# Wider score tiles, a full-array product for the low part of K, and the experts' sums moved by half an item

## The chip, the cores and the metric

The kernel runs on one core of a Trainium2 chip. The metric is the device time of one execution in microseconds. The core has a matrix engine (TensorE, PE in the rows; its weight loads are PEld), VectorE (DVE), ScalarE (ACT), GpSimd (POOL) and SyncE (SP, whose queue issues most DMA transfers); PSUM is the memory that TensorE writes its products to, SBUF the one that all engines work in.

## What is computed

One layer of a hybrid decoder on 2048 tokens of width 1024: a token mixer of three head groups, then a mixture of 32 experts. Three pieces of the reference matter here. The index scores and the sparse attention (n_sel is 256 keys of up to 2048):

```python
logits = jnp.einsum('bqhd,bsd->bqhs', iqb, ikf) * DSA_IDX_DIM ** -0.5      # 8 index heads of 32
score = jnp.einsum('bqh,bqhs->bqs', iwb, jax.nn.relu(logits))
score = jnp.where(admissible[None], score, -jnp.inf)
_, sel = lax.top_k(score, n_sel)
...
s = jnp.einsum('bqhd,bqkhd->bhqk', qb, kg) * DSA_HEAD_DIM ** -0.5          # 4 heads of 64
p = jax.nn.softmax(jnp.where(valid[:, None], s, -jnp.inf), axis=-1)
return jnp.einsum('bhqk,bqkhd->bqhd', p, vg)
```

and the experts, of which every token takes two, with the residual and the final norm:

```python
hid = jax.nn.silu(xb @ w_gate[e]) * (xb @ w_up[e])
return hid @ w_down[e]
...
y = jnp.zeros((T, D), out.dtype).at[tok_sorted].add(contrib)     # contrib: out times the token's weight
...
x = x + gt2 * hier_moe(...)
return rms_norm(x, final_norm_g)
```

## The kernel before

Matrix products are made in a reduced format of f32; for accuracy an operand is split into a high part (ScalarE's copy into that format) and a low part (VectorE's or POOL's difference from it).

*Index scores* (L241 to L264, 60 to 420 us of the span). For a block b of 128 queries the keys up to (b + 1) x 128 are taken in segments of 512. For each pair of segments (GS = 2) and each of 8 heads: one product into a PSUM tile pi (three of 512 columns), a Relu by ScalarE into rl (three of 512) and a multiply-add by VectorE into the sums sb (L253), for each segment by itself; the first head adds to eps, a tiny slope over the keys. Scores of earlier blocks are woven into the projections of later ones; the last blocks stand alone at the end.

*Sparse attention* (L1469 to L1640, 1280 to 1645 us). Query blocks go in pairs; dsa_prep loads the queries of a pair (qd), makes their high part qh on ScalarE, and a tile Q of which, for head parity e, one half of the partitions holds the high part and the other the low part (POOL's difference). dsa_scores multiplies it by KH, which holds the high part of K in both halves (L1533): high times high plus low times high, on all 128 rows. The third term, high times K's low part KL, uses the 64 partitions of that head alone (L1534), so its product has 64 rows. VectorE adds the mask and takes the maximum (L1535), ScalarE makes the exponentials (L1542); dsa_values transposes them (L1565), splits them (ph L1573, pl L1574) and multiplies them by V. Five of the eight 512 KB rows of w_out are loaded meanwhile (NWP = 5), the rest in the output stage.

*Experts* (1930 to 3036 us). The 32 experts' lists have fixed capacities CAP: 18 big items (more than 128 tokens, in two blocks of n rows) alternate with 14 small ones (one block). Step r of the loop works on item r's gate and up products and on item r - 1's down product. A big item does gate and up in two halves of its hidden units (gate_up with c = 0 and 1), and its weights come in 512 KB pieces (slots wraw, 11 of them) that ScalarE and VectorE split into wh and wl (L1904, L1905); a small item multiplies the raw pieces (L1928). In between stands down() for the item before: for the column halves c and the blocks j, 12 products into a PSUM tile pd, VectorE's multiplication by the token's weight and gt2 in place (L1986), and VectorE's addition into part (L1987), the sum so far of these tokens, which POOL gathered from the table yp_d (L1975). POOL scatters part back to yp_d (L1989). finish(), written at the end of the step, squares part on ScalarE (L2000), takes a reciprocal root (two VectorE operations, L61 and L62, and twelve small ones on POOL, L64 to L67), and multiplies part by it and by the final norm's gain into ot on VectorE (L2005), which POOL scatters to the output (L2006). For a token's first expert the sum goes to yp_d only and for its second to the output only; the other scatter leaves that row out. A gather of yp_d waits for the scatters written ahead of it, and a scatter for the one before.

The code is in program order; a scheduler that places instructions by their dependences and expected times sets the order on each engine, so an engine's row is not the order of the code. Engines and queues then run their rows strictly in turn.

## Time and profile before

| | us |
|---|---|
| median of 3 runs | 3036.46 |
| lowest and highest | 3034.36, 3040.60 |
| profiled execution | 3037.47 |
| its span | 3035.6 |
| TensorE busy | 2461.5 (81%) |
| TensorE weight loads | 1884.2 (62%) |
| VectorE busy | 2057.4 (68%) |
| ScalarE busy | 1363.2 (45%) |
| POOL busy | 1074.6 (35%) |

The profile is one execution of the program. An engine is busy while one of its instructions runs; the idle time ahead of an instruction is put down to what released it last ("issue" is a wait for which the profile shows no releaser). The granted clock of TensorE is a share of full speed; its mean over the execution is 0.876.

### The profile page before, as it was taken

Reading aid. Unit: us, or ns where it says so; the run is one execution under the profiler, and the core shown is the slowest. Engines: PE = TensorE matmul, PEld = TensorE weight load, DVE = VectorE, ACT = ScalarE, POOL = GpSimd, SP = SyncE. Lnnn points to the kernel's source line nnn. Section 1 sums busy time; section 2 is a strip of 40 time slices with the busy share of each in tenths; the row PEclk is TensorE's granted clock in tenths of the full one; section 3 lists DMA queues with packets and bytes.
Section 4 is the critical chain, followed back from the end, with each engine's and each line's share of the span. In section 5 each row is a group of like instructions: output and inputs, shape, how many; then the busy total and the mean of one; then the engine's idle time right before and its main releaser. Section 6 shows DMA issues by size and latency. Waiting matters only on the chain.

```text
span 3035.6 us, 39091 instructions
## 1 busy us (share of the span) xinstructions
PE 2461.5 (81%) x12571; PEld 1884.2 (62%) x12571; DVE 2057.4 (68%) x4570; ACT 1363.2 (45%) x2467; POOL 1074.6 (35%) x1123
## 2 busy tenths in 40 slices
PE   4998877778377899789997999488888878887785
PEld 3766645777366677556665788455566655665574
DVE  6588977989879755457676566565566665654575
ACT  2578876663122244356555222243344443443452
POOL 2111133436554332255533354213233333332333
PEclk9999878898667789869998999689999989998888
DMA  7222264433321343353213433687888878887781
GB/s 211 85 91 79 87 224 131 112 132 124 109 84 50 110 144 112 94 147 109 88 49 114 160 133 127 182 250 239 264 258 251 253 234 271 252 245 208 216 235 53
DMA packets 372283, 479.44 MB, mean 158 GB/s; under 512 B 84828, under 2 KB 271356, under 8 KB 371814
## 3 DMA queue, kind: packets, MB, share of 16 engines
q1 hardware_dynamic: 334501, 421.83, 44.5%
q0 software_dynamic: 37568, 55.05, 6.7%
q8 instruction: 100, 1.64, 0.2%
q14 instruction: 114, 0.93, 0.1%
HBM read 385.75 MB, written 112.23 MB: 164 GB/s over the span
## 4 chain that ended last, share of the span: by engine, by line
PE 34%; DVE 11%; DMA 9%; issue 9%; POOL 5%; ACT 3%; SPq 0%; POOLq 0%; ACTq 0%; DVEq 0%
PE pg L1928 6%; DMA wraw<-in_exp_w_down_dram 2%; PE pt L1565 2%; PE ps L1534 2%; DVE wl L1905 2%; PE pw L167 2%; PE pw L166 2%; PE pw L165 2%; DMA part<-yp_d,ix 2%; DMA wraw<-in_exp_w_up_dram 1%; ACT wh L1904 1%; PE ps L1533 1%; PE pd L165 1%; PE pd L167 1%; PE pd L166 1%
## 5 line engine op out<-in xcount | busy, mean ns | idle before, releaser
L1904 ACT ACTIVATE wh<-wraw 128x1024 fp32r<-128x1024 f32 x272 | 285.0, 1054 | 251.2 <-DMA wraw<-in_exp_w_down_dram 93.6
L1905 DVE TENSOR_TENSOR wl<-wraw,wh 128x1024 fp32r<-128x1024 f32 x272 | 330.4, 1220 | 96.7 <-ACT wh L1904 91.9
L1954 PE MATMUL pg<-xT,wh 128*128 128x416 f32 (+10 forms) x1152 | 337.2, 371 | 31.4 <-DVE ga__19052 L1961 5.6
L1928 PE MATMUL pg<-wraw,xT 128*120 128x512 f32 (+9 forms) x448 | 228.2, 670 | 143.5 <-DVE ga__25810 L1961 18.6
L1956 PE MATMUL pg<-xT,wl 128*128 128x208 f32 (+10 forms) x1152 | 288.2, 250 | 0.0
L1928 PEld LDWEIGHTS pg<-wraw,xT 128*120 128x120 f32 (+9 forms) x448 | 86.1, 198 | 276.9 <-issue 114.7
L440 POOL TENSOR_TENSOR xx<-xr,xx 128x1024 fp32r<-128x1024 f32 x64 | 161.7, 2528 | 266.0 <-ACT xx L439 247.0
L1954 PEld LDWEIGHTS pg<-xT,wh 128*128 128x128 f32 x1152 | 230.2, 200 | 40.5 <-DVE ga__19052 L1961 5.8
L1956 PEld LDWEIGHTS pg<-xT,wl 128*128 128x128 f32 x1152 | 233.8, 203 | 0.0
L253 DVE SCALAR_TENSOR_TENSOR sb<-rl,iws,sb 128x512 f32<-128x512 f32 (+3 forms) x266 | 202.1, 808 | 27.3 <-ACT rl L252 23.7
L252 ACT ACTIVATE rl<-pi,iwa 128x512 f32<-128x512 f32 (+3 forms) x304 | 179.1, 653 | 22.4 <-DVE sb L253 16.8
L1863 POOL DMA_INDIRECT xg<-h_d,ix x50 | 53.4, 1068 | 350.7 <-PE pt L1881 329.7
L165 PE MATMUL pp<-xx,w 128*128 128x256 f32 x512 | 154.7, 303 | 21.5 <-ACT ft L486 11.3
L165 PE MATMUL pd<-wh,hid 128*104 128x512 f32 (+17 forms) x400 | 160.6, 402 | 6.6 <-DVE part L1987 4.0
L1989 POOL DMA_INDIRECT yp_d<-part,ix x50 | 70.9, 1418 | 258.8 <-DVE part L1987 189.9
L166 PE MATMUL pd<-wl,hid 128*104 128x512 f32 (+17 forms) x400 | 158.1, 395 | 0.0
L167 PE MATMUL pd<-wh,hid 128*104 128x512 f32 (+17 forms) x400 | 157.5, 394 | 0.0
L166 PE MATMUL pp<-xx,w 128*128 128x256 f32 x512 | 152.2, 298 | 3.1 <-POOL xx L440 3.1
L167 PE MATMUL pp<-xx,w 128*128 128x256 f32 x512 | 151.8, 298 | 0.8 <-POOL w L467 0.8
L250 PE MATMUL pi<-iks,iqs 128*128 128x512 f32 (+3 forms) x304 | 129.2, 478 | 22.2 <-ACT rl L252 19.2
L1535 DVE CUSTOM_DVE_ANT_0 pr<-ps,mk 128x512 f32<-128x512 f32 (+3 forms) x160 | 95.6, 606 | 61.7 <-PE ps L1534 43.5
L165 PE MATMUL pj<-w,xx 128*128 128x512 f32 (+1 forms) x256 | 100.0, 392 | 39.7 <-DVE ot L211 19.5
(1075 smaller groups left out, 7021.8 us busy)
## 6 DMA issues: line engine op xcount, KB each, us to landing
wraw<-in_exp_w_gate_dram SPq DMA_DIRECT2D x128, 512.0 KB
wraw<-in_exp_w_up_dram SPq DMA_DIRECT2D x128, 512.0 KB
wraw<-in_exp_w_down_dram SPq DMA_DIRECT2D x128, 512.0 KB
xr<-hT_d SPq DMA_DIRECT2D x64, 512.0 KB
w<-in_ada_w_dram SPq DMA_DIRECT2D x64, 256.0 KB
w<-in_ada_w_dram SPq DMA_DIRECT2D x16, 512.0 KB
xi<-in_x_dram SPq DMA_DIRECT2D x16, 512.0 KB
hT_d<-ht SPq DMA_DIRECT2D x16, 512.0 KB
```

Source lines behind the costliest of these rows:

```text
L165: TE.matmul(ps, st[0], mv[0], start=(k == first), stop=False, **kw)
L166: TE.matmul(ps, st[0], mv[1], start=False, stop=False, **kw)
L167: TE.matmul(ps, st[1], mv[0], start=False, stop=(k == last), **kw)
L250: TE.matmul(pi[:, :sl], iqs[:, h, i * P:(i + 1) * P], iks[:, s0:s0 + sl], start=True, stop=True)
L252: S.activation(rl[:, :sl], pi[:, :sl], AF.Relu, scale=iwa[:, b, h:h + 1])
L253: V.scalar_tensor_tensor(sb[:, s0:s0 + sl], rl[:, :sl], iws[:, b, h:h + 1], (eps if h == 0 else sb)[:, s0:s0 + sl], op0=OP.mult, op1=OP.add)
L440: G.tensor_sub(xx[1][-1], xr, xx[0][-1].bitcast(F32))
L1904: S.activation(wh, w, AF.Copy)
L1905: V.tensor_sub(wl, w, wh.bitcast(F32))
L1928: TE.matmul(pgs[a][:C], xT[:, kk], wp[2 * i + a][:, k], start=(kk == 0), stop=(kk == KD - 1))
L1954: TE.matmul(pgs[m], wh[:, k, ws], xT[:, i * 4 + k], start=(i + k == 0), stop=False, skip_group_check=True)
L1956: TE.matmul(pgs[m][:, 0], wl[:, k, ws], xT[:, i * 4 + k, 0], start=False, stop=(i + k == 4), skip_group_check=True)
```

## The change

*Scores.* A group of up to 1024 keys is one PSUM tile and one rl tile, two of each; the two products of 512 columns write its halves, and Relu and multiply-add run over the whole width. The modulation's small PSUM tile pr moves into the slot of the projections' tile pp.

```diff
-                for j, (s0, sl) in enumerate(segs[g0:g0 + GS]):
-                    pi = s1p.tile([P, 512], F32, name="pi", bufs=3)
-                    TE.matmul(pi[:, :sl], iqs[:, h, i * P:(i + 1) * P], iks[:, s0:s0 + sl], start=True, stop=True)
-                    rl = ts_.tile([P, 512], F32, name="rl", bufs=RLB)
-                    S.activation(rl[:, :sl], pi[:, :sl], AF.Relu, scale=iwa[:, b, h:h + 1])
-                    V.scalar_tensor_tensor(
-                        sb[:, s0:s0 + sl], rl[:, :sl], iws[:, b, h:h + 1],
-                        (eps if h == 0 else sb)[:, s0:s0 + sl], op0=OP.mult, op1=OP.add)
+                pi = s1p.tile([P, GS * 512], F32, name="pi", bufs=2)
+                for s0 in range(0, gl, 512):
+                    sl = min(512, gl - s0)
+                    TE.matmul(pi[:, s0:s0 + sl], iqs[:, h, i * P:(i + 1) * P], iks[:, g0 + s0:g0 + s0 + sl], start=True,
+                              stop=True)
+                rl = ts_.tile([P, GS * 512], F32, name="rl", bufs=RLB)
+                S.activation(rl[:, :gl], pi[:, :gl], AF.Relu, scale=iwa[:, b, h:h + 1])
+                V.scalar_tensor_tensor(sb[:, gs], rl[:, :gl], iws[:, b, h:h + 1], (eps if h == 0 else sb)[:, gs],
+                                       op0=OP.mult, op1=OP.add)
```

*Sparse attention.* After Q is made, the halves of qh that don't belong to the head are set to zero on POOL; with them the low product takes all 128 rows of KL, of which 64 are multiplied by zeros. qh has two buffers, and NWP falls from 5 to 4.

```diff
-            qh = da.tile([P, 2, 2, 2 * P], F32R, name="qh", bufs=1)
+            qh = da.tile([P, 2, 2, 2 * P], F32R, name="qh", bufs=2)
...
                 G.tensor_sub(Q[l_, e], qd[l_, e], qh[l_, e].bitcast(F32))
+                G.memset(qh[l_, e].bitcast(F32), 0.0)
...
-                    TE.matmul(ps[:, :sl], q_[hs], KL[hs, p_, s0:s0 + sl], start=False, stop=True)
+                    TE.matmul(ps[:, :sl], qz_, KL[:, p_, s0:s0 + sl], start=False, stop=True)
```

*Experts.* down() writes its products into an SBUF tile y (two buffers) and adds nothing. partial() gathers part (three buffers in place of two). add(), half an item later, adds part to y over the full width, tied behind the current item's last hid operation, scatters y, squares y into part and makes the root. finish(), another half item later, multiplies y by root and gain into part and scatters that. The buffers of xg fall from 4 to 3, and the tiles jk and ot are gone.

```diff
-                V.scalar_tensor_tensor(pd[:n], pd[:n], pl[:n, j, 3:4], gt2r[:n, cs], op0=OP.mult, op1=OP.mult)
-                V.tensor_add(parts[j][:n, cs], pd[:n], parts[j][:n, cs])
+                V.scalar_tensor_tensor(ys[j][:n, cs], pd[:n], pl[:n, j, 3:4], gt2r[:n, cs], op0=OP.mult, op1=OP.mult)
+        return ys
...
+            a = V.tensor_add(y[:n], y[:n], part[:n])
+            if after is not None:
+                tc.add_manual_dep(a.ins, after.ins.name, ORDER, reason="products first")
             G.indirect_dma_start(out=yp_d[:, :], out_offset=bass.IndirectOffsetOnAxis(ap=ix[:n, 1, j:j + 1], axis=0),
-                                 in_=part[:n], in_offset=None, bounds_check=T - 1, oob_is_err=False)
+                                 in_=y[:n], in_offset=None, bounds_check=T - 1, oob_is_err=False)
...
-            V.scalar_tensor_tensor(ot[:n], part[:n], rs[:n, j:j + 1], fgr[:n], op0=OP.mult, op1=OP.mult)
+            V.scalar_tensor_tensor(part[:n], y[:n], rs[:n, j:j + 1], fgr[:n], op0=OP.mult, op1=OP.mult)
...
+        if fin is not None:
+            finish(*fin)
         if r:
-            fin = down(sts[r - 1], hid, weights(es_[r - 1], 4))
+            parts = partial(sts[r - 1])
+        if r + 1 < NE:
+            xTn, todo = transpose(CAP[r + 1], sts[r + 1], (r + 1) % 2)
...
+            ys = down(sts[r - 1], hid, weights(es_[r - 1], 4))
         if r < NE:
-            rest()
+            after = rest()
             for f_ in todo:
                 f_()
             if not few:
-                hs.append(gate_up(CAP[r], xT, weights(es_[r], 2), 1))
+                h1, after = gate_up(CAP[r], xT, weights(es_[r], 2), 1)
+                hs.append(h1)
             xT = xTn
             hid = hs
         if r:
-            finish(*fin)
+            fin = sts[r - 1], ys, parts, add(sts[r - 1], ys, parts, after)
+    finish(*fin)
```

How this moves VectorE's row is shown for the big item of 2 x 96 tokens and the small one of 108 that follows it. First the end of the big item's down product, beside the small item's hid and the next item's transposed inputs xT; wl are splits of weight pieces. Before:

```order
L1986 SCALAR_TENSOR_TENSOR pd<-pd,pl_18886,gt2r 96x512
L1939 TENSOR_TENSOR hid<-pt,hid 128x4x108
L1987 TENSOR_TENSOR part<-pd,part 96x512
L1886 TENSOR_TENSOR xT<-pt,xT 128x4x88
L1905 TENSOR_TENSOR wl<-wraw,wh 128x1024
L1986 SCALAR_TENSOR_TENSOR pd<-pd,pl_18886,gt2r 96x512
L1886 TENSOR_TENSOR xT<-pt,xT 128x4x88
L1987 TENSOR_TENSOR part<-pd,part 96x512
L1886 TENSOR_TENSOR xT<-pt,xT 128x4x88
L1905 TENSOR_TENSOR wl<-wraw,wh 128x1024 x2
```

Now:

```order
L1983 SCALAR_TENSOR_TENSOR y<-pd,pl_18386,gt2r 96x512
L1908 TENSOR_TENSOR wl<-wraw,wh 128x1024
L1983 SCALAR_TENSOR_TENSOR y<-pd,pl_18386,gt2r 96x512
L1942 TENSOR_TENSOR hid<-pt,hid 128x4x108
L1889 TENSOR_TENSOR xT<-pt,xT 128x4x88
L2001 TENSOR_TENSOR y<-y,part 96x1024
L1889 TENSOR_TENSOR xT<-pt,xT 128x4x88 x2
L2001 TENSOR_TENSOR y<-y,part 96x1024
L1908 TENSOR_TENSOR wl<-wraw,wh 128x1024 x2
```

The two sums, which followed each product, stand as full-width additions behind all four products and behind hid and the first xT. Next, what follows in VectorE's row: the start of the root (sx, rs_i, rs_y), the norm, and the first ga, a sum that frees the PSUM tiles of the next big item's first half. Before:

```order
L2001 TENSOR_SCALAR sx<-sx 128x2
L61 TENSOR_SCALAR rs_i<-sx 128x2
L62 TENSOR_SCALAR rs_y<-rs_i 128x2
L1905 TENSOR_TENSOR wl<-wraw,wh 128x1024
L2005 SCALAR_TENSOR_TENSOR ot<-part,rs_y,fgr 96x1024 x2
L1961 TENSOR_TENSOR ga__22383<-ga__22383,pg_22349 128x176
L1905 TENSOR_TENSOR wl<-wraw,wh 128x1024
```

Now:

```order
L2010 TENSOR_SCALAR sx<-sx 128x2
L61 TENSOR_SCALAR rs_i<-sx 128x2
L62 TENSOR_SCALAR rs_y<-rs_i 128x2
L1908 TENSOR_TENSOR wl<-wraw,wh 128x1024
L1964 TENSOR_TENSOR ga__21841<-ga__21841,pg_21807 128x176
L2007 MEMSET sx 128x2
L2017 SCALAR_TENSOR_TENSOR part<-y,rs_y,fgr 96x1024 x2
L1964 TENSOR_TENSOR ga__21841<-ga__21841,pg_21808 128x176
L1908 TENSOR_TENSOR wl<-wraw,wh 128x1024 x2
```

The norm (now part, from y) still follows the start of the root; one ga and one operation on sx have moved ahead of it. Last, the small item's end, while the next big item's second half (the later ga) runs. Before, from the small item's second product on:

```order
L1986 SCALAR_TENSOR_TENSOR pd<-pd,pl_18887,gt2r 108x512
L1905 TENSOR_TENSOR wl<-wraw,wh 128x1024
L1987 TENSOR_TENSOR part<-pd,part 108x512
L1905 TENSOR_TENSOR wl<-wraw,wh 128x1024
L2001 TENSOR_SCALAR sx<-sx 128x2
L61 TENSOR_SCALAR rs_i<-sx 128x2
L62 TENSOR_SCALAR rs_y<-rs_i 128x2
L1905 TENSOR_TENSOR wl<-wraw,wh 128x1024
L1961 TENSOR_TENSOR ga__22593<-ga__22593,pg_22559 128x176
L2005 SCALAR_TENSOR_TENSOR ot<-part,rs_y,fgr 108x1024
L1905 TENSOR_TENSOR wl<-wraw,wh 128x1024
```

Now, from the end of that big item's second half on:

```order
L1967 TENSOR_TENSOR ga__22055<-ga__22055,ga__22094 128x2x176
L1969 TENSOR_TENSOR hid<-ga__22055,hid 128x2x176
L2001 TENSOR_TENSOR y<-y,part 108x1024
L2010 TENSOR_SCALAR sx<-sx 128x2
L61 TENSOR_SCALAR rs_i<-sx 128x2
L62 TENSOR_SCALAR rs_y<-rs_i 128x2
L2007 MEMSET sx 128x2
L2017 SCALAR_TENSOR_TENSOR part<-y,rs_y,fgr 108x1024
L1934 TENSOR_TENSOR sg<-sg,pg_22145 112x512
```

The small item's sum, root and norm have moved from the middle of the big item to behind its last hid operation, and stand ahead of sg, the next small item's first operation on VectorE.

## Rows read from the trace of the kernel before

**Rows 1.** Windows by stage: length, busy us by engine, clock, DMA share, GB/s

```profile
60.00:420.00 360.00, 317.49 (x1517) 230.63 (x1518) 284.50 (x495) 266.38 (x544) 70.49 (x91) 0.90 0.28 92
...
1280.00:1645.00 365.00, 333.41 (x1660) 233.53 (x1660) 238.67 (x759) 209.00 (x420) 170.82 (x152) 0.86 0.33 95
...
1930.00:3036.00 1106.00, 886.50 (x4420) 646.17 (x4420) 670.64 (x1073) 447.47 (x717) 355.16 (x584) 0.89 0.78 231
```

**Rows 2.** Windows, the last stretch of the scores

```profile
365.00:420.00 55.00, 40.07 (x71) 19.10 (x71) 51.22 (x70) 45.67 (x75) 13.99 (x11) 0.57 0.47 155
```

**Rows 3.** Groups by line and shape, 60 to 425 us: busy, mean ns, idle

```profile
L253 DVE SCALAR_TENSOR_TENSOR sb<-rl,iws,sb 128x512 f32<-128x512 f32 x196 | 161.1, 865 | 18.5 <-ACT rl L252 17.0
...
L253 DVE SCALAR_TENSOR_TENSOR sb<-rl,iws,eps 128x512 f32<-128x512 f32 x28 | 21.1, 766 | 3.9 <-ACT rl L252 3.9
```

**Rows 4.** Instructions on the tile part, the experts: ns min/median/max

```profile
L2005 DVE SCALAR_TENSOR_TENSOR ot<-part,rs_y,fgr x50: 1274/1281/1290, 2024.1 to 3019.9; 104x1024 f32<-104x1024 f32 x8, 88x1024 f32<-88x1024 f32 x7, 120x1024 f32<-120x1024 f32 x5, 96x1024 f32<-96x1024 f32 x4
```

**Rows 5.** Chain of waits, 1440 to 1640 us: shares by line

```profile
by line: PE pt L1565 20.6%; PE ps L1534 18.9%; PE ps L1533 13.7%; PE po L1556 12.8%; PE po L1555 11.7%; PE ps L137 3.5%; PE pf L1584 3.4%; ACT ph L1573 2.7%; DVE pl L1574 2.0%; POOL KL L1343 1.9%; DVE on L1630 1.8%; ACT pr L1542 1.1%; issue
```

**Rows 6.** The low product's line L1534: idle us, times, by cause

```profile
  issue: 30.5, 121
```

**Rows 7.** Timeline 1560 to 1566 us: start, us, instruction, idle before it

```profile
1562.64 0.39 PE L1533 MATMUL ps<-KH,Q 128*128 128x512 f32 x1
...
1562.96 0.18 PEld L1534 LDWEIGHTS ps<-KL,Q 64*128 64x128 f32 x1 [0.25 <-issue]
...
1563.39 0.42 PEld L1565 LDWEIGHTS pt<-ident,pr 128*128 128x128 f32 x4 [0.25 <-issue]
```

**Rows 8.** Timeline of TensorE, 2262 to 2266 us, a big item's down products

```profile
2263.68 0.40 PE L167 MATMUL pd<-wh,hid 128*96 128x512 f32 x1
2263.92 0.39 PE L165 MATMUL pd<-wh,hid 128*96 128x512 f32 x1
```

**Rows 9.** Groups by line and shape, POOL, whole span

```profile
L290 POOL MEMSET wst<- 128x576 f32 x1 | 0.6, 568 | 0.0
```

**Rows 10.** Waits of VectorE, 1980 to 2990 us: us, times, longest

```profile
DVE sg L1931 <- PE pg L1928: 94.0, 13, 9.3
DVE ot L2005 <- POOL rs_y L67: 90.4, 26, 10.5
DVE wl L1905 <- ACT wh L1904: 79.1, 79, 9.3
DVE part L1987 <- issue: 29.7, 7, 12.4
...
DVE part L1987 <- DMA part<-yp_d,ix: 13.1, 6, 5.7
```

**Rows 11.** The page's costliest groups, small items' gate and up products

```profile
L1928 PE MATMUL pg<-wraw,xT 128*120 128x512 f32 (+9 forms) x448 | 228.2, 670 | 143.5 <-DVE ga__25810 L1961 18.6
```

**Rows 12.** Timeline of VectorE, one pair from 2268 us, and a late one

```profile
2272.68 0.68 DVE L1987 TENSOR_TENSOR part<-pd,part 96x512 f32<-96x512 f32 x1
...
2283.73 0.06 DVE L1997 MEMSET sx<- 128x2 f32 x1 [3.15 <-POOL rs_t L65]
...
2285.12 2.48 DVE L2005 SCALAR_TENSOR_TENSOR ot<-part,rs_y,fgr 96x1024 f32<-96x1024 f32 x2
...
2311.07 1.28 DVE L2005 SCALAR_TENSOR_TENSOR ot<-part,rs_y,fgr 104x1024 f32<-104x1024 f32 x1 [2.60 <-POOL rs_y L67]
...
2754.77 0.69 DVE L1987 TENSOR_TENSOR part<-pd,part 124x512 f32<-124x512 f32 x1 [12.41 <-issue]
```

**Rows 13.** Timeline of POOL, second scatter early, both scatters late

```profile
2279.38 1.56 POOL L1989 DMA_INDIRECT yp_d<-part,ix  x1 [2.82 <-DVE wl L1905]
...
2719.47 1.16 POOL L1989 DMA_INDIRECT yp_d<-part,ix  x1 [0.78 <-DVE part L1987]
...
2729.67 1.16 POOL L1989 DMA_INDIRECT yp_d<-part,ix  x1 [7.48 <-DMA yp_d<-part,ix]
```

**Rows 14.** Timeline of TensorE, the next small item's products

```profile
2313.81 4.54 PE L1928 MATMUL pg<-wraw,xT 128*108 128x512 f32 x10 [1.54 <-DVE ga__22035 L1961]
```

More of the change, by code (lines that the diff above doesn't have):

```diff
@@ L114, in modulate @@
         return acc
-    pr = mps.tile([P, 16], F32, name="pr")
     def modulate_end(q, acc):
@@ L1464, in body @@
     WOK = (0, 1, 2, 5, 6, 7, 3, 4)
-    NWP = 5
+    NWP = 4
     def wo_row(pool, k, **kw):
@@ L1965, in gate_up @@
         S.activation(hid[:, 0], gas[0], AF.Copy)
-        V.tensor_sub(hid[:, 1], gas[0], hid[:, 0].bitcast(F32))
-        return hid
+        return hid, V.tensor_sub(hid[:, 1], gas[0], hid[:, 0].bitcast(F32))
     def down(st, hid, wp):
         n, nb, pl, ix, xgs = st
-        parts = []
-        for j in range(nb):
-            part = mx_.tile([P, D], F32, name="part", bufs=PB)
-            G.indirect_dma_start(out=part[:n], out_offset=None, in_=yp_d[:, :],
-                                 in_offset=bass.IndirectOffsetOnAxis(ap=ix[:n, 0, j:j + 1], axis=0))
-            parts.append(part)
+        ys = [mx_.tile([P, D], F32, name="y", bufs=YB) for j in range(nb)]
         for c in range(2):
@@ L1985, in down, with partial @@
                     mm3(pd[:n], [hid[k // 2][:, z, k % 2, js] for z in range(2)], w, k, 3)
-                V.scalar_tensor_tensor(pd[:n], pd[:n], pl[:n, j, 3:4], gt2r[:n, cs], op0=OP.mult, op1=OP.mult)
-                V.tensor_add(parts[j][:n, cs], pd[:n], parts[j][:n, cs])
-        for j, part in enumerate(parts):
+                V.scalar_tensor_tensor(ys[j][:n, cs], pd[:n], pl[:n, j, 3:4], gt2r[:n, cs], op0=OP.mult, op1=OP.mult)
+        return ys
+    def partial(st):
+        n, nb, pl, ix, xgs = st
+        parts = []
+        for j in range(nb):
+            part = mx_.tile([P, D], F32, name="part", bufs=PB)
+            G.indirect_dma_start(out=part[:n], out_offset=None, in_=yp_d[:, :],
+                                 in_offset=bass.IndirectOffsetOnAxis(ap=ix[:n, 0, j:j + 1], axis=0))
+            parts.append(part)
+        return parts
@@ L1989, in down, with add @@
+    def add(st, ys, parts, after=None):
+        n, nb, pl, ix, xgs = st
+        for j, (y, part) in enumerate(zip(ys, parts)):
+            a = V.tensor_add(y[:n], y[:n], part[:n])
+            if after is not None:
+                tc.add_manual_dep(a.ins, after.ins.name, ORDER, reason="products first")
             G.indirect_dma_start(out=yp_d[:, :], out_offset=bass.IndirectOffsetOnAxis(ap=ix[:n, 1, j:j + 1], axis=0),
-                                 in_=part[:n], in_offset=None, bounds_check=T - 1, oob_is_err=False)
@@ L2001, in finish @@
         V.tensor_scalar(sx, sx, 1.0 / D, EPS, op0=OP.mult, op1=OP.add)
[L2002 to L2005 removed]
+        return rsqrt_(mx_, sx, 2, "rsf", eng=G)
+    def finish(st, ys, parts, rs):
+        n, nb, pl, ix, xgs = st
+        for j, (y, part) in enumerate(zip(ys, parts)):
+            V.scalar_tensor_tensor(part[:n], y[:n], rs[:n, j:j + 1], fgr[:n], op0=OP.mult, op1=OP.mult)
@@ L2044, in body @@
     ahead(1)
-    hid = [None, None]
+    hid, fin = [None, None], None
     for r in range(NE + 1):
+        after = None
         if r < NE:
@@ L2099, in body @@
             rest()
-            finish(*down(st, hid, weights(e, 4)))
+            parts = partial(st)
+            ys = down(st, hid, weights(e, 4))
+            finish(st, ys, parts, add(st, ys, parts))
     es.close()
```

49 lines of the change are left out of this document (21 added, 28 removed).

## The prediction

> **What bounds the kernel now.** I read the table by stage first, then, for each stage that the change touches, the idle time by what ended it, and last the timeline of one repetition. By stage [rows 1] no engine is the bound throughout. The index scores (60 to 420 us) keep TensorE busy for 317.5 of 360 us and VectorE for 284.5; in their last stretch, where little but scores is left, VectorE is busy for 51.2 of 55 us, TensorE for 40.1 at a granted clock of 0.57 [rows 2]. The sparse attention (1280 to 1645) is TensorE's: 333.4 of 365 us against 238.7 on VectorE [rows 1], and over 1440 to 1640 the chain of waits names products and transposes of TensorE for over 80% of the time, L1534 and L1533 for a third [rows 5]. The experts (1930 to 3036) are bound by nothing that a busy share shows (TensorE 886.5, VectorE 670.6 of 1106 us, the DMA engines 78%): they run on a ring. A weight piece has to be split by ScalarE (wh) and VectorE (wl) before its slot is free for the next load, and VectorE takes its instructions in order, so any wait in its row delays loads. TensorE stands before a small item's products (L1928) for 143.5 us in all [rows 11]. VectorE's own waits there are for the norm's reciprocal root from POOL (ot, 90.4 us in 26 waits), for wh (79.1 us) and for gathered sums (part, 29.7 and 13.1 us) [rows 10].
>
> **Part 1, scores by 1024 keys.** Blocks 2 to 15 now make 38 segments of up to 512 keys, times 8 heads 304 Relus and 304 multiply-adds; in groups of up to 1024 they make 22, times 8 is 176. So 128 pairs become one instruction on each of the two engines; the products stay 304. A 512-wide multiply-add takes 766 ns where it reads eps and 865 elsewhere [rows 3], a 1024-wide one of the experts 1281 [rows 4]: two against one save 2 x 0.766 - 1.28 = 0.25 us. Two successive 1024-wide ones take 2.48 us [rows 12], so neighbours overlap by some 0.08 us; counted from start to start, a pair saves 0.17. That is 128 x 0.17 = 22 us of VectorE time, 32 at most, nothing at least. Only the last stretch is VectorE's alone: it holds the last two blocks, 32 pairs, 5 us. Before it TensorE is busier than VectorE and its products don't change, so of the other 17 us I take a third, 5. ScalarE saves about as much but is behind both. The tiles for it, 2 of 1024 for 3 of 512, hold more keys but are handed over in larger steps, which could cost as much as a quarter of what is saved. **-10 us, from -25 to +5.** The modulation's small tile that moves into a slot of the projections: 0 to 1 us, taken as 0.
>
> **Part 2, the low part of K on the whole array.** A pair of 512-wide products now runs so: L1533 starts at 1562.64, the weight load of L1534 only at 1562.96 with 0.25 us of "issue" before it, the next instruction's at 1563.39, again behind 0.25 us of issue [rows 7]: 0.75 us for the pair. The 64-row form has such an idle before it 121 times, 30.5 us [rows 6]. Full-array products of the same 512 columns in the experts start every 0.24 us [rows 8], so a pair would be 0.47 and save 0.28 us; 160 pairs make 45 us of TensorE. The zero rows that it now multiplies add no columns. TensorE is on the chain for 85% of the stretch [rows 5], 38 us; behind it come VectorE's splitting (pl) and ScalarE's ph, which I let end a sixth of what is gained. **-32 us, from -45 to -10.** The Trainium skill (TensorEngine Tiling, Overview and Key Properties) speaks both ways here: a contraction of 64 rows or less is said to gain up to 2x from row tiles that run side by side, which would make the old form the better one, and a change of tiling mode is said to drain the engine. No row here shows two of the 64-row products together, and the idle on both sides of L1534 is what a drain would look like; by the first sentence alone the term would be 0.
>
> The price of the zeros: 16 memsets of 64x512 on POOL. The nearest row, a memset of 128x576, took 568 ns [rows 9]: 9 us on an engine busy for 171 of 365 us [rows 1]. The low product of a block pair's first head waits for one; only the stage's start can feel it, +0.5 us, 8 at most if each pair did. The second qh buffer is paid for with one w_out row that is now loaded and split at the start of the output stage: 512 KB, at the 95 to 231 GB/s of the stages on either side [rows 1] 2 to 6 us, mostly beside other loads, +2. **Together +3.**
>
> **Part 3, experts.** Per block of tokens VectorE's two products in PSUM and two adds (0.68 us each, [rows 12]) become two products into the SBUF tile y and one full-width add. The nearest row for that is ot, 1281 ns over the same 1024 columns with two SBUF operands [rows 4]: 1.28 against 1.36, nothing. The Trainium skill (SBUF — State Buffer, Who interferes with whom) has a rule against such an add: a VectorE instruction with two SBUF inputs contends with a POOL instruction that reads SBUF. If it stretched 50 adds as the common multiply-add of the scores is stretched against the one on eps, 865 to 766 [rows 3], it would cost 50 x 0.17 = 8 us of VectorE. In the experts, beside POOL's own work, ot took 1274 to 1290 ns in all 50 [rows 4], so the sum has none of it.
>
> What counts is where things stand in the rows. *Big item (two blocks).* Its first sum was ready at 2273.36, after the third product and its add; the second scatter started at 2279.38, then came POOL's twelve root steps, and ot at 2285.12 behind a wait of 3.15 us [rows 12, 13]. Now all four products, the small item's hid and one xT stand ahead of the first add, with splits between them: worked out from the durations it ends near 2278.0, 4.6 us later. The second scatter still waits for the first to land, and the norm still stands close behind the root's start in VectorE's row (the order shows it; writing finish half an item later did not move it there). The second scatter's wait of 2.82 us was ended by VectorE's row and not by the landing [rows 13], so some of the 4.6 is slack: ot starts 3.5 us later in early pairs, up to 4.4 in late ones where the scatter is slow. *Small item (one block).* Its two adds (1.36), its stall for the root (2.60) and its ot (1.28, [rows 12]) leave the stretch between the big item's two halves and go behind hid of the second half, where VectorE idles until the next small item's gate products end (sg waits 94.0 us in 13 times, some 7 each [rows 10]). That takes 5.2 us out of the path to the next small item's products at 2313.81 [rows 14] and 3.5 come in; since the loads behind the later ot are issued later too (their slots come free with wl), I leave it a gain of 0.5 us. Eight early pairs: -4.
>
> In the six late pairs the first scatter is slower (2719.47 to 2729.67, 10.2 us [rows 13]) and the stall at a small item's part reaches 12.41 us [rows 12]; of the 42.8 us of waits for part [rows 10] I take all as gone, since the add now stands some 15 us behind its gather: -43. The later norm adds 6 x 4.4 = 26. Two waits are new: the next big item's second product needs the y tile that the small item's scatter reads, and its gather now stands behind that scatter, with a shorter lead; 0 to 3 us a pair, I take 1.5, +9. Late pairs: -8. **-12 us for the experts, from -80 to +70.**
>
> **Sum.** Profiled run 3037.5 - 10 - 32 + 3 - 12 = 2986.5; it lies 1.0 above the median of the runs shown, so 2985.5. Rounded **2986**.
>
> **The rivals.**
> *The experts gain much more.* The path to the next small item is VectorE's row and not the loads; then the 143.5 us before L1928 [rows 11] halve, -72 in place of -12: 2926. For it: what TensorE waits for there is VectorE's ga, and the DMA engines idle for 22%. Against: VectorE waits 79.1 us for wh [rows 10], that is for loads.
> *The attention's gain goes to others.* VectorE and ScalarE take over (pl behind ph behind the transposes), 10 of 32 stay: 3008. For it: VectorE was busy for 239 us of 365 there; against: the chain names TensorE almost alone [rows 5].
> *Slower.* The big item's norm: the first add later by 4.6 us, and behind it the first scatter, the second, the root, ot and every split and load after ot. If nothing on the small side gives it back, 16 pairs x 4.4 = +70: 3036 - 39 + 70 = 3067. It decides from 39 / 16 = 2.4 us per pair. For it: ot's wait for the root is VectorE's second largest [rows 10] and grows; against: 5.2 us leave the same row.
> *Nothing moves.* The parts cancel: 3036.
>
> **How the numbers follow.** Forecast (2955 to 3000) 0.45, large gain 0.20, gain lost in the attention 0.17, slower 0.13, nothing 0.05. A measurement of this kernel tells about 0.2%, 6 us, from no change. Faster 0.82, within 0.2% 0.05, slower 0.13. The range 2920 to 3045 leaves out half of the large gain and most of the slower case, 0.2.
>
> **What would show it.** Right: 176 instructions at the Relu's line; no issue idle before the low product and 0.47 us per pair; the attention 25 to 40 us shorter; part's waits near 0, the wait for the root in big items 3 to 5 us longer, small items' periods about as before. Wrong: the low product as slow on the full array, VectorE idle in new places ahead of y or of the add, or the wait before L1928 halved or grown by more than 30 us.

## The result: 1.4% slower, and the profile after

The changed kernel takes 3080.44 us (median of 4 runs, 3072.31 to 3082.37) against 3035.41 of the kernel before beside it, a ratio of 1.0143 (95% interval 1.0118 to 1.0167). Its profiled span is 3079.0 us against 3035.6. The forecast of 2986 and its range up to 3045 are both missed; of the rivals, "slower" with 3067 comes nearest.

Between landmarks of the two traces the 43.4 us of span divide so (0.4 us lie between them). The last multiply-add of the scores starts 5.3 us earlier (412.0 for 417.3). The sparse attention, from its first product to its last transpose, takes 324.9 us for 355.3, -30.4. The output stage up to the experts' first product (1913.4 for 1943.9) takes 4.8 back. From there to the end: 1165.6 us for 1091.7, **+73.9 in the experts**. The table by stage of the changed kernel, which answers to [rows 1], shows the first two gains as busy time of TensorE and VectorE, and in the experts, over a stretch of the same length, every engine busy for less: they wait more. (Columns as there.)

```profile
60.00:420.00 360.00, 309.80 (x1530) 232.40 (x1530) 272.41 (x389) 250.37 (x419) 71.08 (x91) 0.89 0.29 95
...
1280.00:1645.00 365.00, 291.95 (x1736) 233.67 (x1736) 263.04 (x789) 215.51 (x433) 185.81 (x171) 0.88 0.37 111
...
1930.00:3036.00 1106.00, 877.43 (x4296) 637.35 (x4294) 636.33 (x952) 437.90 (x702) 347.07 (x556) 0.88 0.74 223
```

The low product in the attention, by its line (instructions, ns min/median/max, forms; then the idle time before it by cause), and one pair in the timeline of TensorE:

```profile
L1537 PE MATMUL ps<-KL,qh x160: 224/396/774, 1282.7 to 1592.9; 128*128 128x512 f32 x112, 128*128 128x128 f32 x16, 128*128 128x256 f32 x16, 128*128 128x384 f32 x16
...
  POOL qh L1494: 4.5, 5
```

```profile
1541.70 0.48 PE L1536 MATMUL ps<-KH,Q 128*128 128x512 f32 x1
1542.02 0.39 PE L1537 MATMUL ps<-KL,qh 128*128 128x512 f32 x1
1542.25 0.39 PE L1536 MATMUL ps<-KH,Q 128*128 128x512 f32 x1
1542.48 0.39 PE L1537 MATMUL ps<-KL,qh 128*128 128x512 f32 x1
```

The 121 idle times of kind "issue" [rows 6] are gone, and a pair (1542.02 to 1542.48) takes 0.46 us where it took 0.75 [rows 7].

In the experts, VectorE's waits over 1980 to 2990 us, the view and stretch of [rows 10] (us in total, times, longest):

```profile
DVE wl L1908 <- ACT wh L1907: 170.4, 86, 9.9
DVE sx L2007 <- POOL rs_t L65: 151.3, 28, 12.1
...
DVE y L2001 <- DMA part<-yp_d,ix: 16.7, 6, 7.8
...
DVE part L2017 <- POOL rs_y L67: 13.0, 28, 0.5
DVE sg L1934 <- PE pg L1931: 5.2, 5, 1.5
```

Read them in pairs with those of before. The idle time before sg, VectorE's spare time, is used up: 94.0 to 5.2. The wait for the root is the two POOL lines together, 164.3 us, where it was 111.3 before: 90.4 at ot [rows 10] and this line, in the same stretch:

```profile
DVE sx L1997 <- POOL rs_t L65: 20.9, 5, 7.6
```

So it grew by 53 us. The wait of wl for wh has doubled, 79.1 to 170.4. It is in part a wait for loads: ScalarE's wh itself waited for landing pieces for 157.6 us where it had waited 113.2 (the gate pieces alone 68.1 for 22.9), and some 117 us, where it had been 92, until TensorE's products had freed a buffer. The waits for gathered sums fell from 42.8 to 16.7. On the load queue itself the picture is mixed: its waits that VectorE ended grew from 164 to 223 us at the raw pieces and fell from 497 to 469 at the split ones, 662 to 692 in all. The page's group of the small items' products [rows 11] hardly moved:

```profile
L1931 PE MATMUL pg<-wraw,xT 128*120 128x512 f32 (+9 forms) x448 | 229.1, 675 | 131.1 <-DVE ga__25236 L1964 16.2
```

The pair that [rows 12] and [rows 13] show, in the changed kernel: VectorE first, then POOL (start, us, instruction, idle before it and what ended that).

```profile
2254.32 1.21 DVE L2001 TENSOR_TENSOR y<-y,part 96x1024 f32<-96x1024 f32 x1
...
2256.49 1.21 DVE L2001 TENSOR_TENSOR y<-y,part 96x1024 f32<-96x1024 f32 x1
...
2265.62 0.06 DVE L2007 MEMSET sx<- 128x2 f32 x1 [3.73 <-POOL rs_t L65]
2266.14 2.48 DVE L2017 SCALAR_TENSOR_TENSOR part<-y,rs_y,fgr 96x1024 f32<-96x1024 f32 x2 [0.47 <-POOL rs_y L67]
```

```profile
2255.75 0.98 POOL L1866 DMA_INDIRECT xg<-h_d,ix  x1 [1.99 <-PE pt L1884]
2257.04 1.53 POOL L2004 DMA_INDIRECT yp_d<-y,ix  x1 [0.30 <-issue]
2261.89 0.95 POOL L2004 DMA_INDIRECT yp_d<-y,ix  x1 [3.33 <-DVE ga__21306 L1964]
2262.85 0.22 POOL L64 TENSOR_TENSOR rs_t<-rs_y 128x2 f32<-128x2 f32 x1
...
2265.92 0.19 POOL L67 TENSOR_TENSOR rs_y<-rs_y,rs_t 128x2 f32<-128x2 f32 x1
```

The first sum ends at 2255.53, 15.1 us after the pair's first down product (2240.47); the scatter of it starts at 16.6, behind a gather of the next inputs (xg) that has its own wait; the second scatter at 21.4; then the twelve steps of the root; the norm at 25.7. The row of the second scatter names VectorE's ga as what ended its wait, but ga is not what it needs: the trace has POOL's own wait for the first scatter's landing, and it ended at 2261.14, 0.75 us before the second scatter started. It is so in all 14 pairs of both kernels, with 0.74 to 0.89 us between landing and second scatter, and it holds for the row of 2279.38 in [rows 13] too (landing at 2278.63). Such times, from the first down product, are used below as **places**; means over the 14 pairs:

| place, us | first sum ends | second sum ends | first scatter | second scatter | norm |
|---|---|---|---|---|---|
| before | 11.1 | 15.0 | 11.4 | 19.2 | 24.2 |
| after | 15.5 | 18.7 | 18.2 | 27.0 | 31.3 |

And the stretches of TensorE between one small item and the next, means over 13 periods: the small item's gate and up products, what follows up to the last down product ahead of the next big item's first half (the big item's 48 and the first of the small item's 24: 7 or 8 before, 10 after), that first half, the time up to its second half, that second half, and the pause before the next small item.

| us | small gate | down | half 1 | between | half 2 | pause | period |
|---|---|---|---|---|---|---|---|
| before | 17.3 | 14.8 | 8.8 | 5.4 | 9.9 | 9.6 | 65.8 |
| after | 17.4 | 16.6 | 8.7 | 4.8 | 13.8 | 8.3 | 69.6 |

3.8 us in 13 periods are 49.5; the tail, from the last small item's gate products to the end, takes 225.3 for 198.9, another 26.4. The loss is uneven: single periods change by -2.6 to +11.1 us, and five of them hold 42.8 of the 49.5.

The largest change is in the second halves. Their sums over the 13 periods (us in all, TensorE busy), and two of them each (start and end, length, busy, granted clock, DMA share, GB/s). Before:

```profile
2096.53:2106.42 9.89, 9.89 (x67) 1.00 0.86 253
2290.66:2300.06 9.40, 9.40 (x67) 1.00 0.94 253
sum 128.92, PE 125.17; mean PE 9.63
```

After:

```profile
2066.52:2079.22 12.70, 12.65 (x64) 0.78 0.58 172
2269.52:2279.67 10.15, 9.89 (x67) 1.00 0.76 232
sum 178.93, PE 141.71; mean PE 10.90
```

Of the 50.0 us by which the second halves grew, 33.5 are idle time of TensorE (3.75 to 37.22), all of it ended by VectorE's ga. The other 16.5 are the same products taking longer. The half at 2066.52 ran at a granted clock of 0.78, a mixture of TensorE's two levels of 2.4 and 1.2 GHz, after TensorE had stood idle ahead of it; its first and its last products in the timeline:

```profile
2066.52 0.71 PE L1957 MATMUL pg<-xT,wh 128*128 128x416 f32 x1 [3.31 <-DVE ga__19667 L1964]
...
2067.20 0.59 PE L1957 MATMUL pg<-xT,wh 128*128 128x416 f32 x1
...
2078.76 0.37 PE L1957 MATMUL pg<-xT,wh 128*128 128x416 f32 x1
```

The halves at 2096.53 (the same item before the change) and at 2269.52, with no such idle time ahead of them, ran at 1.00, which is 2.4 GHz throughout.

### The profile page after: what moved, and what is told of

Its sections match the earlier page's. It is cut to its first block, busy times and chain, and to the rows that moved or that the text cites. A ratio compares the mean times of both kernels' runs of the same rounds, so it can differ in the third digit from the quotient of the medians.

```text
span 3079.0 us, 38623 instructions
## 1 busy us (share of the span) xinstructions
PE 2415.8 (78%) x12571; PEld 1885.7 (61%) x12571; DVE 2043.2 (66%) x4392; ACT 1344.5 (44%) x2339; POOL 1095.6 (36%) x1139
## 5 line engine op out<-in xcount | busy, mean ns | idle before, releaser
L2004 POOL DMA_INDIRECT yp_d<-y,ix x50 | 81.8, 1637 | 398.9 <-DVE y L2001 278.1
L255 DVE SCALAR_TENSOR_TENSOR sb<-rl,iws,sb 128x1024 f32<-128x1024 f32 (+7 forms) x154 | 186.6, 1212 | 33.3 <-ACT rl L254 25.0
L162 PE MATMUL pd<-wh,hid 128*104 128x512 f32 (+17 forms) x400 | 165.5, 414 | 40.0 <-DVE y L1983 26.8
L254 ACT ACTIVATE rl<-pi,iwa 128x1024 f32<-128x1024 f32 (+7 forms) x176 | 156.9, 909 | 30.8 <-DVE sb L255 25.3
L162 PE MATMUL pp<-xx,w 128*128 128x256 f32 x512 | 155.4, 304 | 18.3 <-ACT ft L487 10.2
L164 PE MATMUL pd<-wh,hid 128*104 128x512 f32 (+17 forms) x400 | 160.9, 408 | 0.0
L251 PE MATMUL pi<-iks,iqs 128*128 128x512 f32 (+3 forms) x304 | 112.2, 453 | 31.3 <-ACT rl L254 30.4
L2018 POOL DMA_INDIRECT out_dram<-part,ix x50 | 82.6, 1653 | 123.0 <-DMA out_dram<-part,ix 45.5
```

Source lines behind the costliest of these rows:

```text
L162: TE.matmul(ps, st[0], mv[0], start=(k == first), stop=False, **kw)
L164: TE.matmul(ps, st[1], mv[0], start=False, stop=(k == last), **kw)
L251: TE.matmul(pi[:, s0:s0 + sl], iqs[:, h, i * P:(i + 1) * P], iks[:, g0 + s0:g0 + s0 + sl], start=True, stop=True)
L254: S.activation(rl[:, :gl], pi[:, :gl], AF.Relu, scale=iwa[:, b, h:h + 1])
L255: V.scalar_tensor_tensor(sb[:, gs], rl[:, :gl], iws[:, b, h:h + 1], (eps if h == 0 else sb)[:, gs], op0=OP.mult, op1=OP.add)
```

## The experiments

Every comparison is a ratio to the kernel before on the same chip, with its interval. Beside the c runs the kernel before took 3041 us, beside the others 3035 to 3037; so where a c run is set against another run, the difference is that of the ratios, in us of 3036.

**a1, the parts apart: scores and attention alone.** The kernel before with the first two parts of the change.

```diff
+                        TE.matmul(ps[:, :sl], qz_, KL[:, p_, s0:s0 + sl], start=False, stop=True)
+                pi = s1p.tile([P, GS * 512], F32, name="pi", bufs=2)
```

> The scores in 1024 keys and the full-array low product, with the experts of before. Theory (the two early parts gain, the experts' part loses): landmarks of the changed kernel put the scores at -5 us, the attention at -30, the extra w_out row at +5, so about 3005 us, ratio 0.990. Rival (the loss of the experts comes with the earlier parts, for instance by another order of the scheduler): about 3080, or the time of before.

Measured 3002.55, ratio 0.9894 (0.9873 to 0.9916).

**a2, the experts alone.** The kernel before with the third part.

```diff
+            fin = sts[r - 1], ys, parts, add(sts[r - 1], ys, parts, after)
```

> The experts' part alone, scores and attention of before. Theory: the experts take 74 us longer, as between the first gate product and the end in the changed kernel, so about 3110 us, ratio 1.024. Rival: under 3060, if the experts lose only behind the changed earlier parts.

Measured 3105.65, ratio 1.0240 (1.0210 to 1.0269). The product of the two ratios is 1.0131, the whole change's 1.0143: the parts add up, and all of the loss is the experts'.

**c4, the scores alone.**

```diff
+        for g0 in range(0, nk, GS * 512):
+            gl = min(GS * 512, nk - g0)
```

> The scores by 1024 keys alone, with the modulation's tile in the projections' slot. The prediction took 10 us (5 in the last stretch, 5 before it); the last multiply-add of the changed kernel started 5.3 us earlier than before. Theory (in the woven part TensorE sets the pace and the gain is only that of the last stretch): 3 to 7 us, ratio 0.998. Rival: 10 us or more, ratio 0.9967.

Measured 3033.23 against 3041.39, ratio 0.9976 (0.9960 to 0.9992): some 7 us, with 2 to 12 in the interval, so it doesn't separate the two expectations.

**a3, no wait for POOL's root.** The changed kernel with the root of the norm on VectorE, in whose row it stands between sum and norm.

```diff
-        return rsqrt_(mx_, sx, 2, "rsf", eng=G)
+        return rsqrt_(mx_, sx, 2, "rsf")
```

> The changed kernel with the reciprocal root's twelve steps on VectorE in place of POOL, where they stand behind two scatters of which the second waits for the first to land. VectorE stood 178 us before the root's results in the changed kernel (118 before the change). Theory (that wait, in VectorE's row, delays splits and loads and is the loss): the 178 us go, 32 x 12 steps of some 0.2 us = 77 us come, and the time falls by 50 to 100 us, to 2980 to 3030. Rival (the gathers with three xg buffers, the later add or late loads for themselves): 3065 to 3095.

Measured 2963.99, ratio 0.9761 (0.9738 to 0.9783): 116 us below the changed kernel, more than any of the theories asked for.

**a4, the same without the experts' part**, on the kernel of a1.

```diff
-        rs = rsqrt_(mx_, sx, 2, "rsf", eng=G)
+        rs = rsqrt_(mx_, sx, 2, "rsf")
```

> The two early parts, the experts of before, and the root on VectorE. Of the 118 us of VectorE's waits for the root in the kernel before, 77 us of steps take the place. Theory (waits in VectorE's row pass on to loads): 10 to 40 us less than with the root on POOL, 2965 to 2995. Rival (what counts is VectorE's time and not its waits, since the loads follow): the same as with the root on POOL or up to 20 us more.

Measured 2952.25, ratio 0.9722 (0.9697 to 0.9747): 50 us below a1 and below both expectations. So with the root on POOL the old order lost 50 us, and the new one 116. Without it the two orders are 12 us apart instead of 78: the root on POOL carries the loss. The traces say where the 12 us lie: the periods are equal (62.6 us in a3, 62.7 in a4), and the tail takes 205.7 us for 193.3. So the balance of a pair that the prediction worked out, a gain of 0.5 us, comes out close (0.1 us in the traces) once the root is off POOL's row.

**b2 and b3, which items' root.** On VectorE for the two-block items alone, and for the one-block items alone.

```diff
-        return rsqrt_(mx_, sx, 2, "rsf", eng=G)
+        return rsqrt_(mx_, sx, 2, "rsf", eng=None if nb == 2 else G)
```

> The changed kernel with the root on VectorE for the 18 two-block items, on POOL for the 14 one-block items. The prediction put the cost into the two-block items and let the one-block items' root hide in VectorE's idle time ahead of sg. Theory of the prediction: nearly all of the 116 us that the root on VectorE gives, 2960 to 2985. Rival (the one-block items' root, ahead of sg and of the next products' evacuation, costs as much): 3005 to 3040.

```diff
-        return rsqrt_(mx_, sx, 2, "rsf", eng=G)
+        return rsqrt_(mx_, sx, 2, "rsf", eng=G if nb == 2 else None)
```

> The converse: on VectorE for the 14 one-block items, on POOL for the 18 two-block ones. Theory of the prediction: the wait of the two-block items stays, 3055 to 3080. Rival: 3000 to 3040.

Measured 2961.98, ratio 0.9749 (0.9733 to 0.9765), and 3070.11, ratio 1.0113 (1.0084 to 1.0142). The two-block items alone give the whole gain, at the place that the prediction named, the one-block items some 10 us, which is within the two intervals; both are as the theories above had them. VectorE's waits in b2, stretch and columns as above:

```profile
DVE wl L1908 <- ACT wh L1907: 153.3, 87, 10.3
DVE sx L2007 <- POOL rs_t L65: 41.8, 14, 4.3
```

What is left at the root, 41.8 us in 14 times, is the small items'. The period is 62.5 us, half 2 takes 9.9 again and the pause 5.5. In a4, with the old order, the period is as long, with a pause of 9.3: the time that the small item's sum, stall and norm left shows in the pause, and other stretches take it back (the down stretch 16.9 for 14.6).

**b1, the root ahead of the scatters on POOL.** Same engine, other order: the scatters of a norm's sums stand behind its root.

```diff
-            G.indirect_dma_start(out=yp_d[:, :], out_offset=bass.IndirectOffsetOnAxis(ap=ix[:n, 1, j:j + 1], axis=0),
-                                 in_=y[:n], in_offset=None, bounds_check=T - 1, oob_is_err=False)
...
+            tc.add_manual_dep(sc.ins, rsl[-1].ins.name, ORDER, reason="root first")
```

> The changed kernel with the root still on POOL, but its twelve steps tied ahead of the item's scatters, so that they no longer stand behind the second scatter's wait for the first to land. The scatters start some 3 us later. Theory (the loss is the root's place behind the scatters in POOL's row): VectorE's wait for the root falls from 178 us to 32 x 3.3 = 106 us or less, and the time from 3080 to 3000 to 3040. Rival (it is POOL's steps themselves, which VectorE doesn't need once they are its own): within 15 us of 3080.

Measured 3049.19, ratio 1.0038 (1.0024 to 1.0053), outside both expectations, 9 us above the theory's. The norm's place falls from 31.3 to 26.5, as in b2 (26.4), yet the period is 67.8 against b2's 62.5. The scatters come later (first 27.1, second 32.3; b2 19.2 and 29.5), VectorE still idles 89.5 us at the root (of 164.3, in the stretch of [rows 10]), and the small items' products take 19.8 us for 16.6. So the norm's place is not the whole story; a3 and a4 say so too, with the norm at 26.6 and 21.6 and equal periods.

**c1 and c3, the sum's tie.** First the tie kept for one-block items only, so that a two-block item's sums may follow their products again; then the tie taken off the last four items, the tail.

```diff
-            fin = sts[r - 1], ys, parts, add(sts[r - 1], ys, parts, after)
+            fin = sts[r - 1], ys, parts, add(sts[r - 1], ys, parts, after if sts[r - 1][1] == 1 else None)
```

> The changed kernel with the sums tied behind the item's last hid for the 14 one-block items only; for the 18 two-block items the scheduler then puts the first full-width add behind the third product, as before the change, and the first scatter ahead of the gathers of inputs. Root on POOL. In the changed kernel the first add of a two-block item ends 15.5 us after its down products begin (11.1 before the change), the first scatter starts at 18.2 (11.4), the norm at 31.3 (24.2). Theory (this delay, passed on to splits and loads, is the loss of 74 us): the norm back near 25, the time 2990 to 3020. Rival (the one-block items' root, or three buffers of gathered inputs): 3060 to 3085.

```diff
-            fin = sts[r - 1], ys, parts, add(sts[r - 1], ys, parts, after)
+            fin = sts[r - 1], ys, parts, add(sts[r - 1], ys, parts, after if r - 1 < 28 else None)
```

> The changed kernel, root on POOL, with the sums of the last four items alone not tied. From the last one-block item's gate products to the end the changed kernel takes 225.3 us against 198.9 before the change, 26 of the 74 us that the experts lose; the prediction's sum counted pairs and had nothing for this stretch. Theory: 15 to 26 us come back, 3055 to 3065. Rival (the loss there is the late load of weights from the pairs before): within 8 us of 3080.

Measured c1 3061.78, ratio 1.0084 (1.0051 to 1.0117), and c3 3069.05, ratio 1.0091 (1.0062 to 1.0120). c1 is a miss that matters. It undoes the very step that the "slower" rival rests on, the later first sum, and gets back some 18 us (give or take 13), and c3 gives 16 to the tail alone, at the edge of its theory. The traces agree: the tail takes 208.7 us in c1 and 212.4 in c3 for 225.3, the period in c1 69.2 for 69.6. The time lies in the range of c1's rival, but b3 has ruled out one of the rival's two causes, the one-block items' root; the other, three buffers of xg, was not run by itself. The places of c1 say why: sums 11.4 and 16.0, scatters 13.8 and 20.0, nearer to those of before, but the norm at 30.0. Between second scatter and norm lie 10 us in place of 4.3. In POOL's timeline of c1, and VectorE's norm:

```profile
2253.01 1.66 POOL L2004 DMA_INDIRECT yp_d<-y,ix  x1 [1.69 <-DVE sx L2010]
2254.69 1.30 POOL L64 TENSOR_TENSOR rs_t<-rs_y 128x2 f32<-128x2 f32 x1
...
2258.00 0.20 POOL L64 TENSOR_TENSOR rs_t<-rs_y 128x2 f32<-128x2 f32 x1
2260.43 1.02 POOL L1992 DMA_INDIRECT part<-yp_d,ix  x1 [2.24 <-DMA yp_d<-y,ix]
2261.49 0.20 POOL L65 TENSOR_TENSOR rs_t<-rs_t,sx 128x2 f32<-128x2 f32 x1
...
2262.05 0.19 POOL L67 TENSOR_TENSOR rs_y<-rs_y,rs_t 128x2 f32<-128x2 f32 x1
```

```profile
2262.28 1.28 DVE L2017 SCALAR_TENSOR_TENSOR part<-y,rs_y,fgr 96x1024 f32<-96x1024 f32 x1 [6.33 <-POOL rs_y L67]
```

The small item's gather (L1992) has slipped into the big item's root, behind its ninth step. It waits there for the second scatter to land, and the last three steps, 0.75 us from first to last, wait with it.

**d1, that gather behind the root.** c1 with this one order added.

```diff
+            if nb == 1:
+                tc.add_manual_dep(ga_.ins, rsl[-1].ins.name, ORDER, reason="root first")
```

> As the run in which only one-block items' sums are tied, with one order added: the gather of a one-block item's earlier sum (part from the table yp_d) has to stand on POOL behind the whole root of the two-block item before it. In the run without it that gather stands inside the root, behind its ninth of twelve steps in the pair looked at, and waits there 2.24 us for the second scatter's landing; the scatters are 7 us earlier than in the changed kernel, but the norm only 1.3. Theory: this is where the gain of untying went; the norm comes 3 to 4 us earlier in 14 pairs, and the time falls by 30 to 55 us from 3062, to 3005 to 3030. Rival (the norm's place does not set the end any more, the gather's delay gives it back in the small item): 3050 to 3070.

Measured 3026.01, ratio 0.9968 (0.9949 to 0.9987), 35 us below c1, as the theory had it. POOL's timeline of d1 (its line numbers are 2 higher): the root runs through, and the gather waits behind it.

```profile
2241.10 0.19 POOL L69 TENSOR_TENSOR rs_y<-rs_y,rs_t 128x2 f32<-128x2 f32 x1
2242.86 1.84 POOL L1994 DMA_INDIRECT part<-yp_d,ix  x1 [1.57 <-DMA yp_d<-y,ix]
```

The norm's place is 25.4, the period 67.2. With the sums near their old place and nothing inside the root, 54 of the 78 us between the changed kernel and a1 are back; in the traces 18 of them lie in the tail (207.0 for 225.3), which is untied here too, and 31 in the periods. The three buffers of xg are still there, so they can account for the other 24 at most.

**c2, untied sums and no wait for POOL.** c1 and a3 together.

```diff
-        return rsqrt_(mx_, sx, 2, "rsf", eng=G)
+        return rsqrt_(mx_, sx, 2, "rsf")
...
+            fin = sts[r - 1], ys, parts, add(sts[r - 1], ys, parts, after if sts[r - 1][1] == 1 else None)
```

> The same with the root on VectorE. Theory (with the root on VectorE the place of the two-block items' first add matters only where items of two blocks follow each other): as with the untied tail, 2935 to 2950. Rival (an earlier add helps in every pair): under 2930.

Measured 2985.53, ratio 0.9813 (0.9786 to 0.9840): a miss, 16 us *above* a3. The tie is worth something after all. TensorE's largest wait over 1980 to 2850 us in c2, and the same line in a3:

```profile
PE pd L162 <- ACT hid L1941: 36.3, 14, 9.2
```

```profile
PE pd L162 <- ACT hid L1941: 12.0, 13, 1.0
```

An untied sum stands ahead of the last product y and of hid in VectorE's row and stops them when its gather is late; the down stretch takes 18.6 us against a3's 16.9 (and 18.7 in d1). The change's order avoids that, and pays, with the root on POOL, with the place of the root.

**b4, the better version.** a3 with the tail's four items untied, as in c3.

```diff
+        return rsqrt_(mx_, sx, 2, "rsf")
...
+            fin = sts[r - 1], ys, parts, add(sts[r - 1], ys, parts, after if r - 1 < 28 else None)
```

> The changed kernel with the root on VectorE and, for the last four items, which have two blocks and follow each other, the sums not tied behind the next item's last hid. Of the 12 us by which the deferred form with the root on VectorE is slower than the one of before (2964 against 2952), the trace has all in the stretch from the last one-block item to the end (205.7 against 193.4 us). Theory (it is the tie there): 2945 to 2957. Rival (three buffers of gathered inputs or the later norm): within 5 us of 2964.

Measured **2942.43**, ratio 0.9696 (0.9664 to 0.9728), the lowest median of all: 94 us below the kernel before, and 2.6 us below the theory's range. Its tail takes 195 us, a3's 205.7. Its interval overlaps that of a4 (0.9697 to 0.9747): that the experts' new order gains anything over the old one, once the root is on VectorE, is not shown.

## Why the prediction was wrong, point by point

| step | predicted | measured |
|---|---|---|
| scores | -10 | -5.3 in the trace, -7 (-12 to -2) alone (c4) |
| low part of K | -32 | -30.4 |
| memsets, w_out row | +3 | +4.8 (output stage) |
| experts | -12 | +73.9 |

*Scores: right mechanism, too large.* There are 176 instructions, as counted. VectorE's busy time from 60 to 420 us fell by 12.1 us and not by 22. The narrow form was priced by its cheaper kind, 766 ns, although 196 of the 224 full-width ones took 865 [rows 3], and the wide one by the experts' 1281 ns; in the scores it takes more, so that the two errors cancel in part (us busy, mean ns):

```profile
L255 DVE SCALAR_TENSOR_TENSOR sb<-rl,iws,sb 128x1024 f32<-128x1024 f32 x70 | 95.3, 1361 | 10.0 <-ACT rl L254 5.9
...
L255 DVE SCALAR_TENSOR_TENSOR sb<-rl,iws,eps 128x1024 f32<-128x1024 f32 x10 | 15.5, 1550 | 2.5 <-ACT rl L254 2.3
```

*Low part of K: right.* 0.46 us per pair for the 0.47 worked out, and 30 of the 32 us at the end. The sum for it took all 160 pairs as 512 columns wide, and 112 are; what went is as much as the 30.5 us of issue idle of [rows 6]. The memset's price, 519 ns at the median, was bounded well by the 568 of [rows 9], and the products waited for it 4.5 us. By the Trainium skill (TensorEngine Tiling, Overview) alone, which has up to 2x for a contraction of 64 rows or less from smaller tiles, this term would have been 0. It was 30.4 us; here the 64-row product stood alone between full-array ones, and no run has two of them side by side, which is the case of that rule. The rival in which others take the attention's gain did not come.

*A full-width sum from two SBUF tiles: right.* It took 1209 to 1232 ns in all 50, and the norm was as before [rows 4]:

```profile
L2001 DVE TENSOR_TENSOR y<-y,part x50: 1209/1216/1232, 1979.0 to 3052.9; 104x1024 f32<-104x1024 f32 x8, 88x1024 f32<-88x1024 f32 x7, 120x1024 f32<-120x1024 f32 x5, 96x1024 f32<-96x1024 f32 x4
```

*Experts, the big item: the step that failed.* "the first add ... ends near 2278.0, 4.6 us later" was good: 4.4 on average. "ot starts 3.5 us later in early pairs, up to 4.4" was not: 7.1. The prediction read in [rows 13] that the second scatter's wait was ended "by VectorE's row and not by the landing", and took a part of the 4.6 for slack. That reading was wrong: the second scatter started 0.74 to 0.89 us behind the first one's landing in every pair already before the change, so there was no slack, and whatever delays the first scatter delays the root. The 7.1 us are the 4.4 of the sum; 2.4 more ahead of the first scatter, which now stands behind a second gather of the next inputs (xg) that waits for TensorE's transposes (behind one before), and in 5 of 14 pairs waits until a gather of part has landed; 1.0 of a later landing; less 0.6 between second scatter and norm. In all, the root on POOL costs 116 us with the new order (a3) and 50 with the old (a4). So the experts' loss lies in the wait for the root, which the prediction let grow by 3.5 to 4.4 us in a pair and then cancelled against the small item.

*Experts, the small item: the gain that paid for nothing.* The small item's sum, stall and norm did leave their place, and sg's 94.0 us of idle time were filled, as expected. (The products that [rows 14] show at 2313.81 had begun at 2308.52; that row is where they go on after a wait for ga.) But VectorE, late by 7.1 us at the norm, now reaches ga late, and TensorE's second half stops for it and runs at a lower clock: half 2 grew by 3.8 us per period. The down stretch grew by 1.8, of which 0.7 are three more of the small item's products that moved into it from the stretch between the halves, and 0.9 a wait ahead of them for the small item's hid, which all 13 periods have. Against that stand 1.9 gained between the halves and in the pause. The sentence "I leave it a gain of 0.5 us" had the sign wrong with the root on POOL, and the rival "slower" ("If nothing on the small side gives it back") named where the cost would come from. That its price came near was luck: it has 4.4 us in 16 pairs with nothing lost on the way, where the norm came 7.1 later, 3.8 of it reached the period, unevenly, and a third of the loss was the tail; and undoing its step alone (c1) gave little back. It was given 0.13 since two opposed terms of similar size were netted, though one was a wait in VectorE's row and the other time that the next products may not need.

*Late pairs.* Of the 42.8 us of stalls at part, 26 went, not all: 16.7 us of waits for a gather's landing stay. *The tail* has four two-block items in a row and nothing small to give back; it was left out and costs 26.4 us. c3 shows that taking off the tie there returns some 13 to 16.

*The theory that was mended on the way.* That the later sum alone does it fell with c1. Two things act together: the sum's place, and what else stands in POOL's row between it and the end of the root. d1, which puts both nearly back, returns 54 of the 78 us.

*What stays open.* b1, d1 and b2 have the norm at the same place (25.4 to 26.5) and periods of 67.8, 67.2 and 62.5, and a4 has it at 21.6 with 62.7: the norm's place does not set the period by itself. In d1, 1.8 us of the difference to b2 are the down stretch; for b1 the trace shows later scatters and longer small-item products, but no run separates these from VectorE's idle time at the root. A root on VectorE also takes twelve steps out of POOL's row, and so what stands behind them there comes earlier; no run parts that from VectorE's wait. The three buffers of xg for four were not run alone either.

## What to carry to other kernels

When a step moves half an item later on one engine, list what else the *other* engine's row now holds between that step and its consumer: here gathers with waits of their own slipped in front of a scatter and into the middle of twelve tiny operations. A chain of small dependent steps should not share an in-order engine with transfers that wait for landings, if a busy engine waits for its end: the same twelve steps take 2.3 us in VectorE's own row (c2). And a delay in a row that the next products wait for should not be netted against time saved beside it. Last, before part of a delay is called slack, find what the wait really ended with: the name in the row can be that of an instruction that only happened to end then.

## What was not expected of the hardware

A scatter to the table waits on POOL for the one before to land (it starts 0.74 to 0.89 us behind the landing in all 28 pairs of the two traces), and everything in POOL's row waits with it: the means above have 8.8 us between a pair's scatters after and 7.8 before, for an instruction that takes 0.95 to 1.6 us; [rows 13] have 10.2 in a late pair. A root of 12 operations on 128x2 elements takes 3.3 us on POOL when nothing interrupts it and 2.3 us on VectorE (c2). With the root ahead of the scatters on POOL (b1) VectorE's waits for it fall from 164.3 to 89.5 us: nearly half of the wait was for what stood ahead of the root, the rest for its steps. And the same products of a second half took 12.65 us of TensorE at a granted clock of 0.78 (the half at 2066.52, after an idle time of 3.31 us) and 9.89 at 1.00 (the same item's half at 2096.53 before the change).
